# The feed-forward stage of a hybrid decoder step, rebuilt: products in four bank tiles, right operands stored split, and kept sums put back into the banks

## The chip, the cores and the metric

The kernel runs on one core of one Trainium2 chip. The metric is the time of one execution on the device in microseconds (us); lower is better. TensorE is called PE here, its weight loads PEld, VectorE DVE, ScalarE ACT, GpSimd POOL and the sync engine SP, as the profile does.

## The reference, cut to what matters

One layer of a decoder for 512 prompt tokens and 32 sample tokens (544 columns together). The change touches its last block only:

```
hf = rmsnorm(x, norm_ffn_g)
gate, up = split(hf @ w_gate_up, 2)          # 2048 -> 2 x 5632
x = x + (silu(gate) * up) @ w_down           # 5632 -> 2048
```

All is float32. Ahead of it stand the mixers (stick-breaking attention and gated DeltaNet), their output projection and a cross attention; none of that is changed.

## The kernel before, in words

**Products.** The tokens lie as columns: a feature block is a tile of 128 rows by 544 columns, and half of it (272 columns, `HT`) is one half of the tokens. To keep float32 accuracy at the speed of the shorter format `float32r`, each operand is split into two exact parts, `hi` by an ACT copy and `lo` by a DVE subtraction, and a product is three matmuls (hi·hi, hi·lo, lo·hi). On top of that the feed-forward stage uses Winograd's scheme on 2 x 2 blocks: two blocks of weight columns, pairs of feature blocks and the two halves of the tokens give seven products p1 to p7 in place of eight. `wino` (lines 1626 to 1650) runs them: for two pairs at a time it calls `left`, and then issues 7 products x 2 pairs x 3 = 42 matmuls of 128x272. Such a group of 42 is called a step below.

**Left operands.** `left` (lines 1603 to 1623) loads two transfers of 256 KB of weights on SP's queue into a tile `u` (three buffers), makes four sums on POOL (lines 1613 to 1616, 128x256 each), and splits the seven operands in two pieces of 768 and 1024 columns: ACT `wh` (line 1620), DVE `wl` (line 1621). The pieces lie in two pools of two buffers each: the 768 piece holds left operands 0, 1, 2, the 1024 piece 3 to 6. The order of products is p1, p2, p4, p6, p5, p7, p3, which use left operands 1, 2, 0, 4, 3, 5, 6.

**Right operands.** `sums` (lines 1565 to 1576) makes two more tiles from a pair of feature blocks, and `part_of` (lines 1579 to 1592) splits them, so that a pair has seven right operands in seven tiles of 272 KB. `PAIR_TAGS` and `DOWN_PLAN` say in which tiles a pair may lie.

**Banks.** PSUM has eight banks. `wino` takes two tiles of two banks (`mm`: p1, p2 and p6, p5) and three of one bank (`aux`: p4, p7, p3).

**Gate and up.** `ffn` (lines 1682 to 1752) loops over 44 blocks of the hidden features (`j`); each is a `wino` over 8 pairs, so 4 steps. `combine` (lines 1653 to 1680) turns the seven products into gate and up (one ACT copy, seven DVE adds of 128x272 that read a bank), three multiplications on DVE (lines 1712, 1714, 1715) and a Silu on ACT (line 1713) follow. After every second `j` POOL makes the `sums` of the new pair (lines 1572 to 1575), and four transfers on ACT's queue store it, unsplit, in DRAM (`hT`, 7 x 272 columns, lines 1719 and 1721).

**Down.** The 22 pairs of hidden features are taken in chunks of 4, 4, 4, 4 and 6. In a chunk the loop goes over 8 values of `m`, each a `wino` for two blocks of the output: 2 steps, in the last chunk 3. `combine` then adds the chunk's result to two accumulators: one ACT copy, seven DVE adds that read a bank, and two POOL adds of 128x544 (lines 1670 and 1671). `fetch` (lines 1688 to 1699) loads the next chunk's pairs: four transfers on SP's queue (line 1696), seven tiles split by ACT and DVE (lines 1590 and 1591). It is called at m = 4 and m = 10 for one pair each, and at m = 14 for the rest, whose tiles are in use until then. In the last chunk POOL adds the residual x (line 1747), and `store_y` (lines 1767 to 1785) transposes each finished block on PE and stores it.

**Order.** The program is Python that emits instructions; a scheduler orders those of each engine by priority, which is the order of the program unless a block asks for more, and by when their operands and buffers would be free. Each engine then works its list in order: one that waits holds up all behind it.

## Time and profile before

| what | value |
|---|---|
| runs | 3063.03, 3061.66 and 3057.8 us, median 3061.66 us |
| profiled execution | span 3059.9 us, granted PE clock 0.983 |
| feed-forward stage in it | first matmul at 1511.5 us, last one ends at 3048.2 us |
| gate and up | 1511.5 to 2484.3 us: 44 `j`, 176 steps |
| down | 2484.3 to 3048.2 us: 88 steps |
| busy over the span | PE 95%, DVE 70%, POOL 55%, ACT 45% |

A page of the profile shows one execution: busy times by engine, the span in 40 slices, the chain of work that ended last, and the costliest groups of instructions by line. Further views used below cut the span into windows, list who waited for whom, or list the instructions in order of time. Each row names engine, line, operation and tiles; a group ends with its busy time and the mean of one instruction, then with the idle time ahead of it and what ended that.

### The profile page before, as it was taken

How to read it: one execution, taken by the hardware profiler on the slowest of the kernel's cores; microseconds unless marked ns; L12 is line 12 of the kernel's file. 1: busy time of each engine (PE TensorE's matmuls, PEld its weight loads, DVE VectorE, ACT ScalarE, POOL GpSimd, SP SyncE). 2: the span in 40 equal slices, each digit the busy share in tenths (PEclk: the TensorE clock that was granted, in tenths of full speed). 3: DMA queues.
4: the chain of work that ended last, by engine and by line, in shares of the span. 5: the costliest groups of instructions: out<-in, count | busy, mean ns of one | idle time of the engine just before them, and what ended most of it. 6: DMA issues, size and time to landing. Idle time of an engine off the chain costs nothing.

```text
span 3059.9 us, 58347 instructions
## 1 busy us (share of the span) xinstructions
PE 2900.2 (95%) x22118; PEld 2789.1 (91%) x22118; DVE 2134.3 (70%) x3339; ACT 1363.5 (45%) x2600; POOL 1671.8 (55%) x1784
## 2 busy tenths in 40 slices
PE   8999999999999999999799999999999989988898
PEld 7999998889899999999689999999999989988797
DVE  6776775655655655366687777777777888888865
ACT  5544453435645654245543343333333344334333
POOL 3211122312112100032378988898888977999997
PEclk9999999999999999999899999999999999999999
DMA  7323233544535765423434344333434354344343
GB/s 212 95 80 85 75 88 99 144 137 147 173 105 151 227 197 150 127 81 116 161 117 127 118 122 123 121 117 118 125 118 123 116 179 132 110 131 127 119 137 105
DMA packets 619505, 392.67 MB, mean 128 GB/s; under 512 B 36475, under 2 KB 572360, under 8 KB 619224
## 3 DMA queue, kind: packets, MB, share of 16 engines
q1 hardware_dynamic: 596904, 355.95, 39.6%
q10 hardware_dynamic: 22320, 32.99, 3.0%
q8 instruction: 174, 2.85, 0.4%
q14 instruction: 107, 0.88, 0.1%
HBM read 334.17 MB, written 54.68 MB: 127 GB/s over the span
## 4 chain that ended last, share of the span: by engine, by line
POOL 27%; PE 20%; DVE 8%; issue 4%; DMA 4%; ACT 2%; SPq 0%; POOLq 0%; ACTq 0%; DVEq 0%
PE mm L208 7%; POOL u L1615 6%; POOL u L1613 6%; POOL u L1614 5%; PE mm L1647 5%; POOL u L1616 5%; PE aux L1647 4%; DVE wl L1621 3%; DMA u<-in_w_gate_up 2%; DVE pr L1591 2%; PE aux L1342 2%; POOL acc L1670 1%; PE mm L1530 1%; POOL x L1572 1%; PE aux L960 1%
## 5 line engine op out<-in xcount | busy, mean ns | idle before, releaser
L1621 DVE TENSOR_TENSOR wl<-u,wh 128x768 fp32r<-128x768 f32 (+1 forms) x528 | 752.5, 1442 | 315.9 <-ACT wh L1620 213.6
L1647 PE MATMUL mm<-pr,wh 128*128 128x272 f32 x4224 | 830.6, 292 | 41.6 <-DVE acc L1663 25.3
L1620 ACT CAST wh<-u 128x768 fp32r<-128x768 f32 (+1 forms) x528 | 488.8, 943 | 826.5 <-PE aux L1647 295.4
L1647 PEld LDWEIGHTS mm<-pr,wh 128*128 128x128 f32 x4224 | 669.4, 191 | 50.5 <-DVE acc L1663 20.3
L1647 PE MATMUL aux<-pr,wh 128*128 128x272 f32 x3168 | 626.9, 292 | 17.7 <-DVE acc L1669 6.7
L1647 PE MATMUL mm<-pr,wl 128*128 128x272 f32 x2112 | 615.7, 292 | 22.5 <-DVE wl L1621 22.5
L208 PE MATMUL mm<-ah,wh 128*128 128x272 f32 (+1 forms) x2464 | 538.6, 298 | 5.7 <-ACT ah L321 4.6
L1647 PEld LDWEIGHTS aux<-pr,wh 128*128 128x128 f32 x3168 | 506.8, 192 | 21.7 <-DVE acc L1669 8.6
L208 PE MATMUL mm<-al,wh 128*128 128x272 f32 (+1 forms) x2464 | 524.3, 291 | 0.7 <-DVE al L239 0.7
L208 PE MATMUL mm<-ah,wl 128*128 128x272 f32 (+1 forms) x2464 | 515.6, 290 | 0.1
L1647 PE MATMUL aux<-pr,wl 128*128 128x272 f32 x1584 | 460.9, 291 | 2.0 <-DVE wl L1621 2.0
L1647 PEld LDWEIGHTS mm<-pr,wl 128*128 128x128 f32 x2112 | 403.3, 191 | 28.4 <-DVE wl L1621 28.4
L208 PEld LDWEIGHTS mm<-ah,wh 128*128 128x128 f32 (+1 forms) x2464 | 391.9, 189 | 28.8 <-issue 8.5
L197 DVE TENSOR_TENSOR wl<-wr,wh 128x512 fp32r<-128x512 f32 (+1 forms) x366 | 264.0, 725 | 195.9 <-ACT wh L196 186.7
L208 PEld LDWEIGHTS mm<-al,wh 128*128 128x128 f32 (+1 forms) x2464 | 389.6, 188 | 5.4 <-issue 2.0
L208 PEld LDWEIGHTS mm<-ah,wl 128*128 128x128 f32 (+1 forms) x2464 | 386.2, 188 | 2.5 <-DVE wl L197 0.5
L196 ACT CAST wh<-wr 128x512 fp32r<-128x512 f32 (+1 forms) x366 | 224.3, 615 | 336.6 <-PE mm L208 272.6
L1613 POOL TENSOR_TENSOR u<-u 128x256 f32<-128x256 f32 x264 | 277.3, 1050 | 140.8 <-DMA u<-in_w_gate_up 90.2
L1615 POOL TENSOR_TENSOR u<-u 128x256 f32<-128x256 f32 x264 | 323.2, 1224 | 0.0
L1616 POOL TENSOR_TENSOR u<-u 128x256 f32<-128x256 f32 x264 | 308.5, 1169 | 19.1
L1647 PEld LDWEIGHTS aux<-pr,wl 128*128 128x128 f32 x1584 | 303.7, 192 | 2.6 <-DVE wl L1621 2.4
L1614 POOL TENSOR_TENSOR u<-u 128x256 f32<-128x256 f32 x264 | 270.4, 1024 | 0.0
(518 smaller groups left out, 3809.1 us busy)
## 6 DMA issues: line engine op xcount, KB each, us to landing
u<-in_w_gate_up SPq DMA_DIRECT2D x352, 256.0 KB
wr<-in_w_in SPq DMA_DIRECT2D x108, 512.0 KB
u<-in_w_down SPq DMA_DIRECT2D x176, 256.0 KB
v<-hT SPq DMA_DIRECT2D x66, 272.0 KB
page<-in_cache_sb_k SPq DMA_DIRECT2D x128, 128.0 KB
page<-in_cache_sb_v SPq DMA_DIRECT2D x64, 256.0 KB
wr<-in_w_out SPq DMA_DIRECT2D x32, 512.0 KB
hT<-x ACTq DMA_DIRECT2D x44, 272.0 KB
```

What stands on the lines that cost most here:

```text
L196: nc.scalar.copy(hi[:, :m, :n], raw[:, k : k + m, :n])
L197: nc.vector.tensor_sub(lo[:, :m, :n], raw[:, k : k + m, :n], hi[:, :m, :n].bitcast(F32))
L208: c.nc.tensor.matmul(ps[:n, h, :HT], l[:, :n], r[:, h * HT : (h + 1) * HT], start=first and i == 0, stop=last and i == 2,)
L1342: nc.tensor.matmul(ps[:, :256], l, r, start=k == 0 and n == 0, stop=k == 7 and n == 2)
L1591: nc.vector.tensor_sub(lo[:, o : o + n * HT], x[:, : n * HT], hi[:, : n * HT].bitcast(F32))
L1613: nc.gpsimd.tensor_add(s1, a21, a22)
L1614: nc.gpsimd.tensor_sub(s3, a11, a21)
L1615: nc.gpsimd.tensor_sub(s2, s1, a11)
L1616: nc.gpsimd.tensor_sub(s4, a12, s2)
L1620: nc.scalar.copy(hi, u[:, o : o + n])
L1621: nc.vector.tensor_sub(lo, u[:, o : o + n], hi.bitcast(F32))
L1647: nc.tensor.matmul(ps, l[:, cols], r, start=u + i == 0 and j == 0, stop=u + i == n - 1 and j == 2)
```

## The change

1. **Left operands.** Weights and sums get tiles of their own (`raw`, three buffers, and `sum`, two). POOL makes two of the four sums, DVE the other two. The 768 piece is split from `raw` alone.
2. **Banks.** The seven products lie in four tiles that are allocated once: P16 (p1, p6), P7, P45 (p4, p5), P23 (p2, p3). The order of products is p1, p6, p7, p4, p5, p2, p3, so left operands 1, 4, 5, 0, 3, 2, 6. One more bank is left for transposes.
3. **Combination in gate and up.** One ACT copy and five DVE adds (three of 272 columns, two of 544) in place of one and seven.
4. **Right operands of the down projection.** Each pair is split once, before it is stored: ACT makes `hi`, POOL `lo`, and seven transfers of 272 KB on ACT's queue store the tiles. `fetch` is then seven transfers on POOL's queue straight into the operand tiles, and ACT and DVE have no part in it. It asks for the last two pairs of a chunk together.
5. **Accumulation in the down projection.** The seven sums of products of each `m` are kept as they are (`Sums`). After the first chunk ACT puts four of them (P45, P23) back into their banks, and the matmuls add to them; `keep` copies them out again on ACT. P16 and P7 are added on DVE. POOL's two adds by `m` are gone. The combination (`finish`, five DVE adds) runs once, in the last chunk.
6. **Residual.** x is added in the second chunk, with three POOL operations by `m`.

Docstrings and comments, which the change also takes out, are left out here.

```diff
 def left(c, w, k, ca, cb):
-    u = c.wu.tile([P, 8, 2 * P], F32, tag="u", name="u", bufs=3)
+    a, b = (c.wu.tile([P, 4, 2 * P], F32, tag=x, name=x, bufs=n) for x, n in (("raw", 3), ("sum", 2)))
...
-    nc.gpsimd.tensor_add(s1, a21, a22)
-    nc.gpsimd.tensor_sub(s3, a11, a21)
-    nc.gpsimd.tensor_sub(s2, s1, a11)
-    nc.gpsimd.tensor_sub(s4, a12, s2)
+    nc.gpsimd.tensor_sub(b[:, 2], a[:, 0], a[:, 2])
+    nc.gpsimd.tensor_add(b[:, 0], a[:, 0], a[:, 1])
+    nc.vector.tensor_add(b[:, 1], b[:, 2], a[:, 1])
+    nc.vector.tensor_sub(b[:, 3], a[:, 3], b[:, 1])
...
-    todo = ((p1, 1, 0), (p2, 2, 1), (p4, 0, 6), (p6, 4, 4), (p5, 3, 3), (p7, 5, 5), (p3, 6, 2))
+P16, P7, P45, P23 = range(4)
+PRODUCTS = ((P16, 0, 1, 0), (P16, 1, 4, 4), (P7, 0, 5, 5), (P45, 0, 0, 6), (P45, 1, 3, 3), (P23, 0, 2, 1), (P23, 1, 6, 2))
+SEEDED = (P45, P23)
...
+def combine(c, y, z):
+    v = c.nc.vector
+    b, e = c.tt("b"), c.tt("e")
+    s1, u4, u2, u3 = b[:, :HT], b[:, HT:], e[:, :HT], e[:, HT:]
+    c.nc.scalar.copy(s1, c.bank[P16][:, 0])
+    v.tensor_add(u2, s1, c.bank[P16][:, 1])
+    v.tensor_add(u3, u2, c.bank[P7][:, 0])
+    v.tensor_add(u4, u2, c.bank[P45][:, 1])
+    v.tensor_add(halves(z), twice(u3), c.bank[P45])
+    v.tensor_add(halves(y), halves(b), c.bank[P23])
+
+class Sums:
...
+    def seed(self):
+        for p in SEEDED:
+            self.c.nc.scalar.copy(self.c.bank[p], self.parts[p])
+
+    def keep(self, added=False):
+        for p, x in enumerate(self.parts):
+            if added and p not in SEEDED:
+                self.c.nc.vector.tensor_add(x, x, self.c.bank[p])
+            else:
+                self.c.nc.scalar.copy(x, self.c.bank[p])
+
+    def residual(self, y, z):
+        g = self.c.nc.gpsimd
+        g.tensor_add(self.z, self.z, z)
+        g.tensor_add(self.y, self.y, y)
+        g.tensor_sub(self.y[:, HT:], self.y[:, HT:], z[:, HT:])
+
+    def finish(self):
+        v = self.c.nc.vector
+        p1, p6, p7, p5 = self.a[:, :HT], self.a[:, HT:], self.s, self.z[:, HT:]
+        v.tensor_add(p6, p6, p1)
+        v.tensor_add(p7, p7, p6)
+        v.tensor_add(p6, p6, p5)
+        v.tensor_add(halves(self.z), halves(self.z), twice(p7))
+        v.tensor_add(self.y, self.y, self.a)
...
     def fetch(ci, count, got):
-            for i in range(4):
-                n, o = (2, 2 * i - 1) if i else (1, 0)
-                v = c.tk("v") if i % 2 else c.hp.tile([P, T], F32, tag="hv", name="v", bufs=2)
-                nc.sync.dma_start(v[:, : n * HT], src[:, o * HT : (o + n) * HT])
-                part_of(c, v, tags, n, ops)
+            tiles = [operand(c, [tag]) for tag in PAIR_TAGS[DOWN_PLAN[ci][len(got)]]]
+            for i, t in enumerate(tiles):
+                nc.gpsimd.dma_start(t, src[:, i])
...
         if j % 2:
-            dst = hT[j // 2]
-            nc.scalar.dma_start(dst[:, :HT], v[0][:, :HT])
-            for i, x in enumerate((v[1], *sums(c, *v, nc.gpsimd))):
-                nc.scalar.dma_start(dst[:, (2 * i + 1) * HT : (2 * i + 3) * HT], x)
+            tiles = []
+            for i, x in enumerate((*v, *sums(c, *v, nc.gpsimd))):
+                hi, lo, n, _ = part_of(c, x, lambda: c.hp.tile([P, T], F32R, tag="st", name="hs", bufs=4), 2 if i else 1, nc.gpsimd)
+                for t in (hi, lo)[2 - n :]:
+                    nc.scalar.dma_start(hT[j // 2, :, len(tiles)], t[:, :].bitcast(F32))
+                    tiles.append(t)
...
-                if m == KD - 2 and u < 2:
-                    fetch(ci + 1, 1 if len(DOWN_PLAN[ci]) == 4 else 2, nxt)
+                if m == KD - 2 and u == 0:
+                    fetch(ci + 1, 2, nxt)
...
-            p = wino(c, c.w_down, 2 * first[ci], m * P, (m + 1) * P, pairs, step)
             if ci == 0:
-                acc += [c.tt("acc") for _ in range(2)]
+                acc.append(Sums(c, m // 2))
+            else:
+                acc[m // 2].seed()
+            wino(c, c.w_down, 2 * first[ci], m * P, (m + 1) * P, pairs, step, 0, SEEDED if ci else ())
+            acc[m // 2].keep(ci > 0)
+            if ci == 1:
+                x = [c.cst.tile([P, T], F32, tag="rstd", name="xl", bufs=2) for _ in range(2)]
+                for i in range(2):
+                    nc.sync.dma_start(x[i], c.xT[m + i])
+                acc[m // 2].residual(*x)
             if last:
-                x = c.wu.tile([P, 2, T], F32, tag="u", name="xl", bufs=3)
-                nc.sync.dma_start(x, c.xT[m : m + 2].rearrange("k p t -> p k t"))
-                for i in range(2):
-                    nc.gpsimd.tensor_add(acc[m + i], acc[m + i], x[:, i])
-            combine(c, p, *acc[m : m + 2], None if ci == 0 else nc.vector if last and m == KD - 2 else nc.gpsimd)
-            if last:
-                done = [(m + i, acc[m + i]) for i in range(2)]
+                acc[m // 2].finish()
+                done = [(m, acc[m // 2].y), (m + 1, acc[m // 2].z)]
...
+    banks = ctx.enter_context(tc.tile_pool(name="banks", bufs=1, space=PSUM))
+    c.bank = [banks.tile([P, n, 512], F32, name=f"bank{i}")[:, :, :HT] for i, n in enumerate((2, 1, 2, 2))]
+    c.aux = lambda: banks.tile([P, 512], F32, tag="aux", name="aux", bufs=1)
     ffn(c, pairs, st, r1)
```

More of the change, by code (lines that the diff above doesn't have):

```diff
@@ L1646, in wino @@
                 for j, (l, r) in enumerate(((wh, bh), (wh, bl), (wl, bh))):
-                    nc.tensor.matmul(ps, l[:, cols], r, start=u + i == 0 and j == 0, stop=u + i == n - 1 and j == 2)
+                    nc.tensor.matmul(
+                        c.bank[p][:, o], l[:, cols], r,
+                        start=u + i == 0 and j == 0 and p not in seeded, stop=u + i == n - 1 and j == 2,
+                        skip_group_check=p in seeded,
+                    )
         if step:
             step(u // 2)
-    return p1, p2, p3, p4, p5, p6, p7
```

97 lines of the change are left out of this document (38 added, 59 removed).

## The prediction, made blind

> **What bounds the kernel now.** I read the page first, then windows along the stages, then who waited for whom, then the groups by shape. A step is 42 matmuls, a `j` of gate and up 4 steps, an `m` of the down projection 2 (3 in the last chunk).
>
> ```profile
> PE 2900.2 (95%) x22118; PEld 2789.1 (91%) x22118; DVE 2134.3 (70%) x3339; ACT 1363.5 (45%) x2600; POOL 1671.8 (55%) x1784
> POOL 27%; PE 20%; DVE 8%; issue 4%; DMA 4%; ACT 2%; SPq 0%; POOLq 0%; ACTq 0%; DVEq 0%
> ```
>
> PE is busiest over the span, yet the chain that ended last runs through POOL more than through PE. The windows say where (PE, PEld, DVE, ACT, POOL busy; then granted clock, DMA share, GB/s):
>
> ```profile
> 1511.50:1596.80 85.30, 72.23 (x513) 69.70 (x514) 72.56 (x91) 45.75 (x70) 61.93 (x58) 0.92 0.41 127
> 1596.80:2484.30 887.50, 870.91 (x6890) 864.29 (x6889) 685.82 (x744) 342.92 (x418) 792.84 (x736) 1.00 0.40 122
> 1877.30:1899.30 22.00, 21.25 (x170) 21.00 (x169) 16.33 (x19) 8.19 (x10) 18.28 (x19) 1.00 0.43 133
> 1899.30:1920.40 21.10, 21.10 (x170) 21.10 (x169) 16.81 (x19) 8.40 (x10) 20.79 (x19) 1.00 0.37 109
> 2484.30:2582.30 98.00, 88.00 (x675) 86.27 (x674) 84.53 (x113) 45.87 (x65) 77.46 (x72) 0.97 0.50 150
> 2582.30:2677.10 94.80, 88.85 (x674) 87.66 (x673) 80.48 (x101) 39.68 (x55) 85.11 (x73) 0.96 0.42 123
> 2633.60:2644.10 10.50, 10.50 (x86) 10.50 (x85) 8.79 (x13) 4.16 (x5) 10.42 (x9) 1.00 0.37 108
> 2677.10:2785.10 108.00, 90.96 (x675) 88.86 (x673) 94.86 (x111) 42.37 (x60) 105.38 (x85) 0.93 0.43 126
> 2785.10:2887.60 102.50, 89.65 (x672) 87.69 (x672) 88.36 (x106) 40.23 (x57) 99.26 (x82) 0.95 0.42 125
> 2887.60:3048.20 160.60, 146.21 (x1074) 140.96 (x1075) 102.76 (x117) 60.47 (x111) 142.28 (x119) 0.94 0.43 126
> 3048.20:3059.90 11.70, 3.04 (x16) 2.20 (x14) 4.48 (x10) 3.58 (x13) 0.00 (x0) 0.67 0.25 74
> ```
>
> Row 7 is one undisturbed `m`: two steps in 10.50 us, 5.25 a step, the pace of PE's matmuls. At that pace the first three `j` would take 63 us (row 1: 85.3), the other 41 would take 861 (row 2: 887.5, 21.65 each; an even `j` 22.0 and an odd one 21.1, rows 3 and 4), and the 88 steps of the down projection 462 (rows 5, 6 and 8 to 10: 563.9). So the matmuls are at their pace in gate and up, and the excess of 102 us lies in the down projection, at a clock of 0.93 to 0.97 with POOL almost without a pause (99.26 of 102.5). After the last matmul 11.7 us are left.
>
> **POOL's relief.** Its groups from 2582.3 to 2887.6 us, chunks 1 to 3:
>
> ```profile
> L1613 POOL TENSOR_TENSOR u<-u 128x256 f32<-128x256 f32 x48 | 47.6, 991 | 8.7 <-DMA u<-in_w_down 7.5 <-DVE acc L1669 1.2
> L1614 POOL TENSOR_TENSOR u<-u 128x256 f32<-128x256 f32 x48 | 57.8, 1204 | 0.0
> L1615 POOL TENSOR_TENSOR u<-u 128x256 f32<-128x256 f32 x48 | 55.8, 1163 | 0.0
> L1616 POOL TENSOR_TENSOR u<-u 128x256 f32<-128x256 f32 x48 | 51.6, 1076 | 3.8
> L1670 POOL TENSOR_TENSOR acc<-acc,a 128x544 f32<-128x544 f32 x23 | 49.0, 2130 | 0.0
> L1671 POOL TENSOR_TENSOR acc<-acc,b 128x544 f32<-128x544 f32 x23 | 35.4, 1540 | 3.0 <-DVE b L1668 3.0
> ```
>
> Four adds twice and the two accumulations make 2 x 4.43 + 3.67 = 12.5 us for an `m` that PE does in 10.5: POOL can't make up for any delay. After the change two adds a step are left, 4.9 us at the dearest mean, in the second chunk three operations more (about 2 x 2.1 + 1.2). POOL stops being the bound there.
>
> **DVE's load in gate and up** is the price. What a moved add costs is bounded by the same add of 272 columns on both engines, and by a DVE group that always met POOL and one that never did:
>
> ```profile
> L1613 POOL TENSOR_TENSOR u<-u x264: 716/742/1866, 1489.6 to 3031.1; 128x256 f32<-128x256 f32 x132
> L1572 DVE TENSOR_TENSOR x<-v x8: 430/435/1024, 1481.6 to 1541.7; 128x272 f32<-128x272 f32 x8
> L1675 DVE TENSOR_TENSOR g<-b,mm x44: 419/430/432, 1550.7 to 2492.5; 128x272 f32<-128x272 f32 x44
> L1714 DVE TENSOR_TENSOR u<-u,rstd x44: 1247/1258/1270, 1553.3 to 2495.0; 128x544 f32<-128x544 f32 x44
> L1670 DVE TENSOR_TENSOR acc<-acc,a x1: 721/721/721, 3051.9 to 3051.9; 128x544 f32<-128x544 f32 x1
> L1621 DVE TENSOR_TENSOR wl<-u,wh 128x1024 fp32r<-128x1024 f32 x264 | 415.0, 1572 | 254.2 <-ACT wh L1620 152.4 <-POOL u L1614 96.4 <-PE aux L1647 4.2
> L1621 DVE TENSOR_TENSOR wl<-u,wh 128x768 fp32r<-128x768 f32 x264 | 346.5, 1312 | 61.7 <-ACT wh L1620 61.2
> ```
>
> With a bank as one input the duration never varies (419 to 432 ns); with two tiles of SBUF it lies between 430 and 1024, and 544 columns take 721 ns at the end, where POOL has no work, against 1258 beside it. So the two engines hold each other up. From 430 and 721 a column costs 1.07 ns, so 768 and 1024 columns undisturbed about 0.96 and 1.24 us (estimates); the means hold 0.35 and 0.33 us of waiting. That is 2.7 us a `j`, with the multiplications about 4.
>
> A `j` gains eight DVE adds: 3.4 us at 0.43, 8.2 at 1.02. POOL's own work at its cheapest falls from 16 x 0.73 + 1.5 (a pair's sums, as two such adds) = 13.2 us to 8 x 0.73 + 1.5 + 2.7 (the new `lo` parts, 952 columns a `j` at 0.73 for 256) = 10.0, so I let DVE's waits shrink by a quarter, 1.0 us, and take 0.6 for an add, near its undisturbed row: 4.8. The new combination takes 3 x 0.43 + 2 x 0.72 against 7 x 0.43, 0.3 less. From 16.8 (row 4): 16.8 + 4.8 - 1.0 - 0.3 = 20.3 of 21.0. DVE is then nearly full, and it works in order:
>
> ```profile
> ACT wh L1620 <- POOL x L1575: 134.1, 18, 7.7
> DVE wl L1621 <- ACT wh L1620: 108.6, 132, 2.6
> ```
>
> (waits in row 2's window.) The first is the even `j`: the store of the sums sits in ACT's queue waiting for POOL, with the next weights' casts behind it, up to 7.7 us. Seven stores that wait for POOL's `lo` parts replace four; POOL is freer. I let half of the 1 us go. The new order of products also frees the 768 piece after 36 of 42 matmuls in place of 18, so a late split has 6.0 us before PE needs it where it had 8.3, and the 1024 piece 6.0 for 7.5. For that and the fuller DVE I add 0.25 us: 21.5 a `j`, 881.5 for 41. Bounds: 21.0, and 16.8 + 8.2 - 0.3 = 24.7. The first three `j` stay at 85.3: the same splits of the tokens fill them.
>
> Two-tile DVE operations and POOL exclude each other in the Trainium skill too, for the whole of an instruction (SBUF — State Buffer, section "Who interferes with whom"). By that rule with undisturbed durations an odd `j` would have needed 13.2 + 8.8 + 2.2 = 24.2 us; the trace has 21.1, so only part of each instruction excludes the other. Taken as it stands it gives 24 after the change as well (10.0 + 8.8 + 2.2 + 3.4), so 21.65 would stay and the sum would be 6 us higher.
>
> **The put-back sums.** ACT's copies:
>
> ```profile
> L1661 ACT COPY g<-mm x44: 377/386/388, 1545.4 to 2487.0; 128x272 f32<-128x272 f32 x44
> L1713 ACT ACTIVATE g<-g x44: 647/652/660, 1554.6 to 2496.7; 128x544 f32<-128x544 f32 x44
> PE mm L1647 <- DVE acc L1663: 25.3, 12, 7.4
> ```
>
> No row writes a bank from ACT; I take 0.65 us for 544 columns in either direction, as the second row, which is nearest; 0.39 for half of them bounds it below, the last rival but one above. P45 ends 12 matmuls (1.5 us) before the `m` does and is wanted 18 (2.25) into the next: 3.75 us for 1.3 us of copies. P23 has 30 matmuls, 3.75 us too. One pair of casts ahead of them (8.40 us a `j`, so 2.1 a step at most) still fits: 3.4. They are hidden; if not, each of 32 `m` waits. In exchange PE's waits for the accumulation (third row, down projection) go: P16 is complete 30 matmuls before the end.
>
> **The fetch at a chunk's start.** Two pairs, 14 tiles of 272 KB, 3.9 MB, must come between the end of the last `m`'s first step and the second step of the next chunk: 10.5 us.
>
> ```profile
> q1 hardware_dynamic: 596904, 355.95, 39.6%
> q10 hardware_dynamic: 22320, 32.99, 3.0%
> ACT pr L1590 <- DMA v<-hT: 36.7, 20, 6.2
> 2677.10:2699.40 22.30, 13.94 (x87) 13.21 (x85) 21.93 (x25) 9.00 (x14) 22.06 (x17) 0.77 0.56 163
> ```
>
> q10 carried these long rows: 32.99 MB in 3.0% of the span, 359 GB/s when working; q1 mostly weights, 294. So 10.9 us, 3.6 for two steps of weights, 1.8 for the landing (third row, mean): 16.3, 5.8 late, and 2 us for the slow clock after a pause (fourth row: 0.77): 8 a chunk. Chunk 0 needs four pairs and waits 10. The last needs four as well, 10, and in seven of its `m` the transposes stay:
>
> ```profile
> 3008.42 0.63 PE L960 MATMUL aux<-ident,acc 128*128 128x128 f32 x4
> 3009.03 0.40 PE L1781 MATMUL aux<-ident,acc 128*32 128x128 f32 x2
> 3010.44 0.52 PE L1647 MATMUL aux<-pr,wh 128*128 128x272 f32 x2 [1.01 <-DVE acc L1669]
> ```
>
> From 3008.35 to 3010.44 no product runs, with four more transposes 2.4 us, of which 1.0 is a wait that I keep, since one bank is left for them. Of the 14 issues for the two early pairs of a chunk (m = 4 and 10) nothing shows: POOL has 5 us free in each `m`. The stores grow from 0.95 to 1.9 MB for two `j`, 23 GB/s at a DMA share of 0.40; hidden. Down: 94 + 3 x 92 + (126 + 10 + 16) = 522, against 563.9.
>
> **End and sum.** Behind the last matmul seven adds of 0.43 and two of 0.72 become one copy and one add: 11.7 - 3.0 = 8.7. 1511.5 + 85.3 + 881.5 + 522 + 8.7 = 3009.0, 50.9 under the span of 3059.9. The runs' median, 3061.66, less that is 3010.8.
>
> **Rivals.** DVE becomes the bound of gate and up: an add at 0.73, the middle of its bounds, no relief in the old waits, and half of the 2.6 us a `j` that it waits for ACT stay: 16.8 + 5.8 - 0.3 + 1.3 = 23.6, so 3097; it ends slower than before from 22.75 a `j` on, 3142 at 24.7. For it speaks 20.3 of 21.0, against it POOL's lighter load.
>
> The fetch through POOL's queue is no faster than the old path: each issue holds POOL and the adds behind it, waits for a tile to come free included. SP's issue takes about 0.34 us; at 1.2 us 14 take 17, and each start costs about 9 more: 3056. In the Trainium skill a transfer from this queue takes 2.0 us and its bytes at 436 GB/s (DMA: Bandwidth & Descriptors, "Anatomy of one DMA — SWDGE (gpsimd) path"), 2.6 us for a tile; 14 without overlap would be 37 us. No run here shows one.
>
> The put-back holds PE: a copy behind casts that themselves wait for PE, 1.9 us for 32 `m`: 3072.
>
> Everything hides: 21.1 a `j`, 4 us a start, the first `j` 10 us shorter: 2965.
>
> **Numbers.** Forecast 0.44, all hidden 0.18, DVE 0.20, POOL's queue 0.12, put-back 0.06. A measurement of this kernel can tell about 0.2%, 6 us. Faster: 0.44 + 0.18 + most of POOL's queue, 0.70; same 0.07; slower 0.23. The range reaches from all hidden, 2960, into the DVE case, 3090; alone the forecast has 2985 to 3040.
>
> **What would show it.** Down windows near 92 us with POOL well under 90% busy and a clock near 1; no wait of PE on an accumulation. Gate and up: DVE above 90%, a `j` near 21.5. Wrong, if a `j` takes over 22.5 with PE waiting for `wl`, if PE waits for the fetched tiles over 10 us a chunk, or if it waits for ACT's copies at each `m`.

## The result and the profile after

After takes 3131.11 us (median of 4 runs, 3128.71 to 3132.79), before in the same series 3062.35 (4 runs): a ratio of 1.0231, 95% interval 1.0216 to 1.0246. That is slower by 2.3%, outside the forecast's range and on its other side. The profiled execution of after has a span of 3131.0 us, 71.1 more than before's.

The page of after, busy times and the chain that ended last:

```profile
PE 2925.2 (93%) x22118; PEld 2814.3 (90%) x22118; DVE 2168.3 (69%) x3513; ACT 1441.3 (46%) x2720; POOL 1042.2 (33%) x1444
PE 36%; DVE 12%; POOL 7%; issue 4%; DMA 4%; ACT 2%; ACTq 0%; SPq 0%; POOLq 0%; DVEq 0%
```

POOL lost 630 us of work and its share of the chain fell from 27% to 7%, as meant. Still the kernel is slower, so shares over the span can't tell why. The windows by stage can (PE, PEld, DVE, ACT, POOL busy; granted clock, DMA share, GB/s): first three `j`; `j` 3 to 42; one even `j`; one odd `j`; the last `j`; chunks 0 to 4; what follows the last matmul.

```profile
1514.40:1602.20 87.80, 74.19 (x513) 71.80 (x514) 72.16 (x106) 43.64 (x67) 42.48 (x41) 0.91 0.34 107
1602.20:2567.20 965.00, 888.88 (x6723) 878.34 (x6722) 773.11 (x963) 377.38 (x481) 441.81 (x480) 0.96 0.41 129
2009.00:2036.00 27.00, 23.06 (x170) 22.62 (x169) 20.69 (x25) 10.09 (x14) 14.82 (x15) 0.94 0.45 142
2036.00:2057.10 21.10, 21.10 (x171) 21.10 (x169) 18.11 (x25) 8.76 (x12) 7.50 (x10) 1.00 0.38 112
2567.20:2602.20 35.00, 23.51 (x170) 23.21 (x169) 18.51 (x22) 8.83 (x12) 23.07 (x40) 0.80 1.07 309
2602.20:2696.30 94.10, 87.81 (x675) 87.14 (x674) 62.26 (x70) 48.42 (x68) 44.06 (x63) 0.95 0.57 166
2696.30:2789.70 93.40, 87.47 (x675) 84.90 (x674) 79.72 (x78) 46.58 (x65) 65.40 (x76) 1.00 0.69 202
2789.70:2882.70 93.00, 86.78 (x675) 86.40 (x674) 63.51 (x80) 46.57 (x65) 43.11 (x66) 0.96 0.67 192
2882.70:2970.40 87.70, 85.57 (x674) 84.36 (x674) 63.73 (x80) 46.69 (x65) 39.63 (x62) 1.00 0.64 185
2970.40:3118.80 148.40, 137.57 (x1076) 135.69 (x1075) 108.51 (x153) 72.97 (x129) 41.64 (x61) 0.95 0.47 137
3118.80:3131.00 12.20, 3.21 (x16) 1.57 (x14) 2.06 (x4) 3.94 (x13) 0.00 (x0) 0.71 0.24 71
```

The balance against before, in us: start of gate and up +2.9, first three `j` +2.5, `j` 3 to 42 +99 (965.0 against 865.8), the last `j` +13.3 (35.0 against 21.7), down projection -47.3 (516.6 against 563.9), end +0.5: together 71. The odd `j` is undisturbed (21.1, clock 1.00). The loss is in the even `j`, right after a pair is complete: 27.0 us against 22.0, twenty times. It lies in the third of the four steps, 11.3 us in place of 6.3 (means of the twenty).

Who waited for whom in `j` 3 to 42 (engine and line, releaser, us in total, times, longest), of PE, ACT and POOL:

```profile
PE bank L1654 <- ACT wh L1624: 55.9, 20, 3.2
ACT hs L1594 <- POOL hs L1595: 114.7, 40, 4.9
POOL sum L1617 <- DVE wl L1625: 498.3, 160, 5.6
```

Twenty waits of PE for ACT's cast of the weights (and 22, 20.0 us in all, for VectorE's split of them), forty of ACT for a low part that POOL makes. The timeline of `j` 20 shows how the two hang together (start, us, engine, line, operation; in brackets the idle time before it). POOL, then ACT, then PE:

```profile
2014.84 1.16 POOL L1617 TENSOR_TENSOR sum<-raw 128x256 f32<-128x256 f32 x1 [5.37 <-DVE wl L1625]
2015.95 0.74 POOL L1618 TENSOR_TENSOR sum<-raw 128x256 f32<-128x256 f32 x1
2016.65 0.95 POOL L1573 TENSOR_TENSOR x<-u 128x272 f32<-128x272 f32 x1
2017.57 0.95 POOL L1574 TENSOR_TENSOR x<-u,x 128x272 f32<-128x272 f32 x1
2018.60 1.37 POOL L1575 TENSOR_TENSOR x<-u,x 128x272 f32<-128x272 f32 x1
2019.93 1.33 POOL L1595 TENSOR_TENSOR hs<-u,hs 128x544 fp32r<-128x544 f32 x1
...
2016.11 5.51 ACTq L1760 DMA_DIRECT2D hT<-hs  x2
2021.66 0.64 ACT L1594 CAST hs<-x 128x544 fp32r<-128x544 f32 x1 [4.85 <-POOL hs L1595]
2022.21 1.04 ACT L1624 CAST wh<-sum 128x1024 fp32r<-128x1024 f32 x1
...
2023.30 0.52 PE L1654 MATMUL bank<-pr,wh 128*128 128x272 f32 x2 [2.91 <-ACT wh L1624]
```

Read it backwards. PE waits at 2023.30 for the cast at 2022.21. The sums were ready (VectorE's last add of them ended at 2017.89), but the cast stands in ACT's queue behind two stores, and the second store waits 5.5 us for a low part that POOL finishes at 2021.26. POOL had been idle for 5.37 us before 2014.84; then sums of weights, three of the pair's sums and the low part came all at once. The load of no engine shows this: POOL is busy 14.82 of 27.00 us.

Before has the same wait in ACT's queue, and a longer one. A row of its timeline, from `j` 22:

```profile
2018.18 3.47 ACT L1620 CAST wh<-u 128x1024 fp32r<-128x1024 f32 x4 [7.44 <-POOL x L1575]
```

What differs is when it ends. From the first matmul of an even `j` to the weights' cast behind the long store it is 11.1 us in before and 13.4 in after (means of the twenty), while the third step begins at 10.5 in both. PE idles 0.8 us in an even `j` of before and 3.8 in one of after. The other 2.0 of the 5 us are in the matmuls themselves: behind the pause they ran at a lower granted clock, 0.77 in the row below and 1.00 in the odd `j`, and PE is busy 23.06 us in this `j` against 21.10 in the next.

```profile
2023.30:2030.75 7.45, 6.42 (x37) 6.20 (x37) 5.97 (x5) 3.11 (x4) 3.45 (x5) 0.77 0.45 161
```

The last `j` is another matter, also on POOL: it issues transfers of the fetch, many of which wait for their tile, and the next weights' sums stand behind them (the first and the last row of those that hold the 28 issues, the sum behind them, and PE's wait in that `j`):

```profile
2568.01 1.30 POOL L1735 DMA_DIRECT2D pr<-hT  x2 [1.76 <-PE bank L1654]
...
2590.96 0.53 POOL L1735 DMA_DIRECT2D pr<-hT  x1 [0.24 <-DMA pr<-hT]
2591.50 0.73 POOL L1617 TENSOR_TENSOR sum<-raw 128x256 f32<-128x256 f32 x1
...
PE bank L1654 <- ACT wh L1624: 11.5, 1, 11.5
```

### The profile page after: what moved, and what is told of

Read it like the earlier page. It is cut to its first block, busy times and chain, and to the rows that moved or that the text cites. A ratio compares the mean times of both kernels' runs of the same rounds, so it can differ in the third digit from the quotient of the medians.

```text
span 3131.0 us, 58882 instructions
## 1 busy us (share of the span) xinstructions
PE 2925.2 (93%) x22118; PEld 2814.3 (90%) x22118; DVE 2168.3 (69%) x3513; ACT 1441.3 (46%) x2720; POOL 1042.2 (33%) x1444
## 3 DMA queue, kind: packets, MB, share of 16 engines
q1 hardware_dynamic: 584360, 334.50, 36.8%
## 4 chain that ended last, share of the span: by engine, by line
PE 36%; DVE 12%; POOL 7%; issue 4%; DMA 4%; ACT 2%; ACTq 0%; SPq 0%; POOLq 0%; DVEq 0%
PE bank L1654 24%; PE mm L208 7%; DVE wl L1625 6%; POOL sum L1617 2%; PE aux L1342 1%; DVE sum L1619 1%; DMA raw<-in_w_gate_up 1%; DMA raw<-in_w_down 1%; POOL hs L1595 1%; PE mm L1530 1%; ACT wh L1624 1%; POOL x L1575 1%; PE aux L960 1%; DMA pr<-hT 1%; POOL x L1573 1%
## 5 line engine op out<-in xcount | busy, mean ns | idle before, releaser
L1654 PE MATMUL bank<-pr,wh 128*128 128x272 f32 x7392 | 1444.0, 295 | 105.3 <-ACT wh L1624 88.4
L1654 PEld LDWEIGHTS bank<-pr,wh 128*128 128x128 f32 x7392 | 1196.8, 194 | 115.5 <-ACT wh L1624 96.5
L1654 PE MATMUL bank<-pr,wl 128*128 128x272 f32 x3696 | 1089.4, 295 | 30.3 <-DVE wl L1625 30.1
L1654 PEld LDWEIGHTS bank<-pr,wl 128*128 128x128 f32 x3696 | 717.7, 194 | 38.8 <-DVE wl L1625 38.0
L1617 POOL TENSOR_TENSOR sum<-raw 128x256 f32<-128x256 f32 x264 | 221.4, 839 | 786.4 <-DVE wl L1625 748.3
L1625 DVE TENSOR_TENSOR wl<-sum,wh 128x1024 fp32r<-128x1024 f32 x264 | 334.3, 1267 | 105.6 <-ACT wh L1624 103.6
L1624 ACT CAST wh<-raw 128x768 fp32r<-128x768 f32 x264 | 220.0, 833 | 366.2 <-PE bank L1654 328.1
L1619 DVE TENSOR_TENSOR sum<-sum,raw 128x256 f32<-128x256 f32 x264 | 233.8, 886 | 164.3 <-POOL sum L1617 164.1
L1625 DVE TENSOR_TENSOR wl<-raw,wh 128x768 fp32r<-128x768 f32 x264 | 280.0, 1061 | 73.2 <-ACT wh L1624 46.7
L1624 ACT CAST wh<-sum 128x1024 fp32r<-128x1024 f32 x264 | 277.2, 1051 | 104.6 <-DVE sum L1620 95.0
L1618 POOL TENSOR_TENSOR sum<-raw 128x256 f32<-128x256 f32 x264 | 209.4, 793 | 0.0
L1735 POOL DMA_DIRECT2D pr<-hT x154 | 83.0, 551 | 33.1 <-PE bank L1654 16.6
```

The source lines that it names most:

```text
L1617: nc.gpsimd.tensor_sub(b[:, 2], a[:, 0], a[:, 2])
L1618: nc.gpsimd.tensor_add(b[:, 0], a[:, 0], a[:, 1])
L1619: nc.vector.tensor_add(b[:, 1], b[:, 2], a[:, 1])
L1624: nc.scalar.copy(hi, x)
L1625: nc.vector.tensor_sub(lo, x, hi[:, :, :].bitcast(F32))
L1654: nc.tensor.matmul(c.bank[p][:, o], l[:, cols], r, start=u + i == 0 and j == 0 and p not in seeded, stop=u + i == n - 1 and j == 2, skip_g ...
```

## The experiments

Durations are taken from each run's profiled execution: a `j` from its first matmul to the next one's (mean of the twenty even ones from 4 to 42, of the twenty odd ones from 3 to 41), the down projection as a whole. Ratios are to before, measured beside each run. In the diffs `...` marks what is left out, and comments are added here.

| run | us | ratio, 95% interval | even `j` | odd `j` | last `j` | down |
|---|---|---|---|---|---|---|
| before (profiled) | 3062.35 | 1 | 22.2 | 21.1 | 21.7 | 563.9 |
| after | 3131.11 | 1.0231 (1.0216-1.0246) | 27.2 | 21.1 | 35.1 | 516.6 |
| x1_stores_pool | 3137.16 | 1.0270 (1.0253-1.0287) | 27.0 | 21.9 | 36.3 | 513.8 |
| x2_stores_sp | 3119.99 | 1.0207 (1.0190-1.0224) | 26.0 | 22.1 | 36.3 | 514.2 |
| x3_order | 3207.74 | 1.0497 (1.0479-1.0514) | 26.4 | 24.7 | 36.8 | 535.3 |
| x4_lo_dve | 3064.46 | 1.0020 (1.0009-1.0031) | 24.0 | 21.3 | 37.6 | 515.4 |
| y1_lo_dve_st_sp | 3080.64 | 1.0074 (1.0054-1.0094) | 24.2 | 21.9 | 35.9 | 514.4 |
| y7_spread | 3143.14 | 1.0275 (1.0253-1.0297) | 27.2 | 21.8 | 35.4 | 517.3 |
| y5_left_dve_at_fetch | 3054.54 | 0.9991 (0.9981-1.0002) | 24.0 | 21.3 | 24.6 | 516.8 |
| y4_fetch_sp | 3054.85 | 0.9995 (0.9986-1.0004) | 24.0 | 21.3 | 33.8 | 508.4 |
| y6_no_putback | 3137.23 | 1.0257 (1.0236-1.0278) | 27.2 | 21.1 | 34.7 | 526.4 |
| z1_sum3 | 3341.86 | 1.0935 (1.0918-1.0952) | 29.4 | 24.3 | 21.2 | 625.5 |
| x6_left_pool | 3197.35 | 1.0461 (1.0446-1.0477) | 29.3 | 21.1 | 38.1 | 536.9 |
| z3_mix | 3043.36 | 0.9960 (0.9947-0.9973) | 23.6 | 21.1 | 24.4 | 516.7 |
| w1_no_lo | 3080.18 | 1.0082 (1.0066-1.0097) | 24.2 | 22.2 | 36.4 | 507.8 |
| z4_lo_in_place | 3114.71 | 1.0192 (1.0178-1.0206) | 26.6 | 21.4 | 28.4 | 515.3 |
| z6_fetch_sp | 3049.34 | 0.9965 (0.9953-0.9977) | 23.5 | 21.1 | 21.1 | 522.3 |
| v1_whole | 3034.17 | 0.9923 (0.9910-0.9936) | 23.8 | 21.1 | 25.0 | 501.5 |
| v2_whole_pool | 3036.01 | 0.9922 (0.9909-0.9935) | 23.9 | 21.1 | 24.4 | 503.3 |

**First theories: a queue, the buffers, or VectorE.** The stores moved to SyncE's queue:

```diff
-                    nc.scalar.dma_start(hT[j // 2, :, len(tiles)], t[:, :].bitcast(F32))
+                    nc.sync.dma_start(hT[j // 2, :, len(tiles)], t[:, :].bitcast(F32))
```

> The same stores issued from SP's queue, where the loads of the weights stand. Queue theory: ACT is free as in the kernel with the stores on POOL's queue, but now the weights' loads wait behind stores that wait for POOL's lo parts; three raw buffers cover about two steps (10.5 us), so between 3030 us (covered) and 3090 (half of the stall moves to the loads). DVE theory and buffer theory: about 3131.

The even `j` kept 26.0 us, and the odd one rose by 1.0. PE's long wait for ACT's cast is gone, and its third step falls from 11.3 us to 8.5. But the weights' cast still stands behind ACT's cast of the pair, which waits for POOL's sums, and VectorE's split behind it takes 2.17 us beside POOL's low parts (1.22 where POOL is idle). PE waits for that split, 1.69 us in each of the twenty. In `j` 10 of this run:

```profile
1773.12 0.65 ACT L1594 CAST hs<-x 128x544 fp32r<-128x544 f32 x1 [1.73 <-POOL x L1574]
1773.67 1.04 ACT L1624 CAST wh<-sum 128x1024 fp32r<-128x1024 f32 x1
1774.75 2.17 DVE L1625 TENSOR_TENSOR wl<-sum,wh 128x1024 fp32r<-128x1024 f32 x1 [0.85 <-ACT wh L1624]
1775.80 3.62 POOL L1595 TENSOR_TENSOR hs<-x,hs 128x544 fp32r<-128x544 f32 x2
1776.98 0.59 PE L1654 MATMUL bank<-pr,wl 128*128 128x272 f32 x1 [1.69 <-DVE wl L1625]
```

On SyncE's queue the stores hold raw weights besides: POOL waited for these 20 times, 69.6 us in all, and the fourth step and the next odd `j` got longer.

The stores on POOL's own queue (x1_stores_pool, the same line with `nc.gpsimd`) were to bring 100 us if ACT's queue was the cause. The even `j` kept 27.0 us; PE's waits are for VectorE's splits here too, among them 1.69 us at the same place in all twenty. That the store's wait in ACT's queue is the whole cause fell with these two runs. What they leave is that the weights' casts and splits stand behind work of the pair that waits for POOL; neither run takes all of that away.

An order of the products like that of before, in which the 768 piece is used up earlier:

```diff
-PRODUCTS = ((P16, 0, 1, 0), (P16, 1, 4, 4), (P7, 0, 5, 5), (P45, 0, 0, 6), (P45, 1, 3, 3), (P23, 0, 2, 1), (P23, 1, 6, 2))
+PRODUCTS = ((P16, 0, 1, 0), (P45, 0, 0, 6), (P23, 0, 2, 1), (P16, 1, 4, 4), (P7, 0, 5, 5), (P45, 1, 3, 3), (P23, 1, 6, 2))
```

> The changed kernel with the products in another order (p1, p4, p2, then p6, p7, p5, p3), so that the 768 piece is free after 18 of 42 matmuls again, as before the change, and a late split has 8.3 and 7.5 us in place of 6.0. Buffer theory: the even j comes back to about 22 us, 3030. Queue theory: the stall of 6 us shrinks by the 1.5 to 2.3 us of slack, 20 x 2 = 40 us less, 3090. DVE theory: 3131. In the down projection the banks have less time between their last and their next matmul, which may cost some us there.

The even `j` gained 0.8 us, every odd one lost 3.6. In this run PE waits for no cast and no split of the weights in gate and up, although these come as late as in after (13.8 us from the start of an even `j`). Its waits are for banks:

```profile
PE bank L1654 <- DVE e L1673: 110.1, 38, 5.0
```

So going back to an earlier order doesn't bring the 5 us back, since the lateness reaches PE by VectorE's combination instead. But the time that an order leaves until PE wants a late piece does decide whether it waits for it; the buffer theory is not refuted as a part of the cause.

The low parts of the stored pairs on VectorE:

```diff
-... "st", name="hs", bufs=4), 2 if i else 1, nc.gpsimd)
+... "st", name="hs", bufs=4), 2 if i else 1, nc.vector)
```

> The changed kernel with the lo parts of the stored pairs made by DVE in place of POOL (1904 columns for two j, about 2.7 to 4.5 us). Queue theory: the first three stores of a pair no longer wait for POOL, the last four still wait for POOL's sums: an even j falls by about half of the stall, 24 us, so about 3070. DVE theory: DVE gets fuller and the even j longer, 3150 or more.

67 us come back by giving the engine said to be nearly full more work: the whole loss against before but 0.2%. So VectorE was not the bound, and the engine that makes the low parts decides most of it. The mechanism stays, but shorter: in `j` 20 of this run ACT's first two stores wait 3.35 us in place of 5.51, and the weights' casts go on after 11.6 us in place of 13.4. The third step still takes 7.0 to 9.2 us.

With the low parts on VectorE and the stores on SyncE's queue as well (y1_lo_dve_st_sp) the even `j` is no better, 24.2, and the time 3080.64 us: POOL now waits for raw weights, 20 times, 72.2 us in all.

**The order of the same work.** The pair's sums, parts and stores handed out in four pieces, one behind each of the next four steps:

```diff
-            for i, x in enumerate((*v, *sums(c, *v, nc.gpsimd))):
...
+            later = pair_out(c, hT, j // 2, v)     # a generator of four pieces
...
+        def step(u):
+            next(later, None)
```

> After with the same instructions on the same engines and queues; only their order is changed: the stored pair's second half (sums, casts, low parts, stores) is not issued in one piece behind the pair, but in four pieces, one behind each of the next j's four weight steps. Burst theory (eight instructions in one piece stand in POOL's and ScalarE's in-order queues ahead of the next steps' weight sums and weight casts): an even j falls from 27.1 us to 21.3 to 22.3, about twenty of them, 3131 - 20 x 5.3 = 3020 to 3035; j 43 and the chunk starts stay. Capacity theory (POOL, at 14.8 us busy of an even j's 27, or VectorE has no room wherever the work stands): nothing moves, 3125 to 3135, or the loss goes over to the other three steps. Theory of the buffers (four st buffers for seven stored tiles, each waiting for a landed store): spreading gives the stores time, so it would also fall, but to 23 to 24: 3060 to 3075.

Nothing was gained. POOL's low parts now lie apart, with weight sums between them, yet the first store still waits 5.51 us and the cast behind it is as late (`j` 22 of this run, ACT):

```profile
2067.02 5.51 ACTq L1731 DMA_DIRECT2D hT<-hs  x2
2072.58 1.04 ACT L1624 CAST wh<-sum 128x1024 fp32r<-128x1024 f32 x1 [4.85 <-POOL hs L1595]
```

The first three sums and the first low part still came in one piece, so the theory was half tested: what it says of the later pieces is refuted, what it says of the first is not touched.

**More buffers for the weight sums**, three in place of two:

```diff
-    a, b = (... for x, n in (("raw", 3), ("sum", 2)))
+    a, b = (... for x, n in (("raw", 3), ("sum", 3)))
```

> After with three buffers in place of two for the weight sums; the room comes from letting three operand tiles of one gate/up pair share one tile, so that part of the operands (and so of the result) is overwritten; the number of instructions and matmuls is that of after. Before had three buffers for raw blocks and sums together, after has three for the raw blocks but two for the sums, and POOL waits 5.4 us per j for a sum buffer just ahead of the burst. Lookahead theory (the third step's sums could have been made in that wait, and then the burst would hit nothing): even j falls from 27.1 to 22 to 23.5, 3131 - 20 x 4 = 3040 to 3060. Queue theory (ScalarE's casts stand behind stores that wait for POOL's low parts, whatever is ready ahead): an even j falls by 2 us at most, 3085 to 3131.

Both theories missed: 3341.86 us, every stage but the last `j` slower. The down projection says nothing on buffers here: the three operand tiles that share one are also tiles that a fetch fills, so its transfers can have to wait for one another. `j` 3 to 42 have no such transfers, and took 1073.6 us in place of 965.0. POOL and VectorE waited there:

```profile
POOL sum L1621 <- DMA raw<-in_w_gate_up: 496.3, 90, 8.2
DVE sum L1623 <- POOL sum L1621: 286.3, 140, 4.6
```

With room for a further sum, VectorE's queue holds the sum of a later step ahead of the low part of the current one, and so waits for weights that are still loading, while their buffer waits for VectorE. The waits are shown; that this order is their cause is read from one stretch of the timeline, and was not tested by itself.

**The split of the weight sums.** All four on POOL again, nothing else changed:

```diff
-    nc.vector.tensor_add(b[:, 1], b[:, 2], a[:, 1])
-    nc.vector.tensor_sub(b[:, 3], a[:, 3], b[:, 1])
+    nc.gpsimd.tensor_add(b[:, 1], b[:, 2], a[:, 1])
+    nc.gpsimd.tensor_sub(b[:, 3], a[:, 3], b[:, 1])
```

> After with the first part undone alone: all four weight sums on POOL, everywhere, as in the kernel before; the low parts of the stored pairs stay on POOL. If POOL's work in an even j is the cause (14.8 us busy there, and 8 x 0.8 more make 21.2 of 21.1): even j 28 to 30, and the down projection loses part of its 47 us, since POOL then carries four sums a step: 3170 to 3230. If the cause is that the sums now pass from POOL to VectorE, which adds a wait of POOL and one of VectorE to every step, and not the low parts: even j back to 22 to 24, 3050 to 3090.

Slower by another 66 us: 2.1 in each even `j`, 20 in the down projection. With the low parts on POOL, the split of the sums is needed.

**The put-back**, taken out: VectorE adds all kept sums.

```diff
-SEEDED = (P45, P23)
+SEEDED = ()
```

> After without the put-back: all kept sums are added to their banks' products by VectorE, none is put back by ScalarE. It prices the part that the change is named for. If the put-back only moves work that is hidden either way (VectorE is busy 63.7 of a chunk's 87.7 us, and 2 x 0.71 us an output pair more make it 75): 3125 to 3137. If the bank's release behind four adds in a row is late for the next output pair's matmuls: 0.6 to 1 us for each of 32 output pairs, 3150 to 3163. If the put-back itself costs: down to 3110.

The ratio's interval overlaps after's; the profile has 9.8 us more in the down projection (526.4), 5.4 of them in chunk 3. The part that gave the change its name is worth about 10 us at most, and costs nothing.

**The last `j` and the chunk starts.** On top of x4_lo_dve, VectorE makes POOL's two sums in the last `j` and in the first and last `m` of each chunk:

```diff
+    eng = eng or nc.gpsimd          # nc.vector if j == NH - 1, or m in (0, KD - 2)
-    nc.gpsimd.tensor_sub(b[:, 2], a[:, 0], a[:, 2])
-    nc.gpsimd.tensor_add(b[:, 0], a[:, 0], a[:, 1])
+    eng.tensor_sub(b[:, 2], a[:, 0], a[:, 2])
+    eng.tensor_add(b[:, 0], a[:, 0], a[:, 1])
```

> The kernel with the low parts on VectorE (3064), and also, in the three kinds of blocks around a fetch of stored pairs (the last j, and the first and last output pair of each chunk), the two weight sums that POOL makes are made by VectorE, so that no weight sum stands behind POOL's transfer issues. Theory that POOL's in-order queue makes the loss there (j 43 37.6 us in place of 21.1, the second step of chunk 2's and chunk 4's first output pair 8 and 13 us too long): j 43 falls to 22 to 26, the chunk starts to within 3 us, together 20 to 30 us: 3035 to 3045. Theory that the raw weights land late beside the fetch's transfers: j 43 stays over 32, and under 8 us come back: 3056 to 3064. VectorE being overrun instead (2 x 0.8 us more in each of those steps) would show as steps of 5.5 to 6 us in all of those blocks: 3060 to 3075.

The last `j` falls from 37.6 to 24.6: POOL's queue was most of the cause there. The down projection doesn't fall (516.8 against 515.4), so there the theory failed: PE's waits for ACT's casts shrink from 15.6 us to 2.1, but it now waits longer for VectorE's additions to the kept sums (7.3 us, 3.7 in x4_lo_dve) and for the fetched tiles themselves (3.4 there, here):

```profile
PE bank L1655 <- DMA pr<-hT: 8.4, 6, 4.9
```

On top of x4_lo_dve again, with the sums left on POOL and the fetches on SyncE's queue:

```diff
-                nc.gpsimd.dma_start(t, src[:, i])
+                nc.sync.dma_start(t[:, :].bitcast(F32), src[:, i])
```

> After with the low parts on VectorE (alone 3064) and the fetches of stored pairs on SyncE's queue in place of POOL's, so that no weight sum on POOL stands behind a fetch. If POOL's queue makes the loss at the last j (37.6 us against 21.3) and at the chunk starts: j 43 under 26, chunk 2 and 4 each 5 us shorter, 3035 to 3050. If the raw weight loads, now behind fetches that wait for their tiles in SyncE's queue, are late instead: j 43 30 or more and chunks of 95 to 100, 3065 to 3090.

The down projection gains 7 us, the last `j` only 3.8, because raw weights now stand behind the fetches: SyncE issues 26 of them from 2504.58 to 2524.28, and the next raw block at 2524.66, for which POOL waits until 2531.49.

**Mixing engines.** Low parts on VectorE, all four weight sums of gate and up on POOL, and y5's sums around the fetches:

```diff
+        wino(..., eng=(nc.vector,) if j == NH - 1 else (nc.gpsimd, nc.gpsimd))   # engines of the first and last two sums
```

> Low parts of the stored pairs on VectorE; in gate/up all four weight sums on POOL (as in the kernel before), which gives VectorE 1.3 to 1.7 us of every step back; around the fetches the POOL sums on VectorE as in the run that gave 3054.5; the rest of the down projection as in after. If what is left of an even j's loss there (23 to 25 us against 21.1) is VectorE, full in the third step: even j 21.5 to 22.5, 3005 to 3025. If POOL's four weight sums with the pair's four sums make a new burst: even j 23 to 25 again or more, 3050 to 3075. The last j and the chunk starts stay at the values of the 3054.5 run (24.6 us; 8 us each, PE waiting for fetched tiles).

Faster than before by 0.4%, but the even `j` stayed at 23.6: VectorE's load was not what was left. In the profile its low part of the pair waits for ACT's cast, 2.07 us at 1985.62, with the weights' low part behind it. z6_fetch_sp puts the fetches of chunks 1 to 4 on SyncE's queue, and POOL's two sums of the down projection back on POOL:

> The kernel that gave 3043 with the fetches for chunks 1 to 4 from SyncE's queue and POOL's two weight sums back on POOL in the down projection. If POOL's queue made part of the chunk starts' loss: the down projection 505 to 510 in place of 516.7, 3030 to 3038. If the fetched data are late whoever asks for them: 3040 to 3047. If raw weights now wait behind fetches: 3050 or more.

No gain (0.9965 against 0.9960): chunks 2 and 3 fell by 7 and 3 us, but the first step of chunk 0 took 26.7 us in place of 6.9, more than the last `j` gained (21.1 in place of 24.4). That wait only moved.

**The low parts left out** (high parts stored twice in their place, so that the down projection lacks the low ones; stores and buffers stay, and ACT makes one more copy of 272 columns for each pair):

```diff
-                hi, lo, n, _ = part_of(...)
-                for t in (hi, lo)[2 - n :]:
...
+                nc.scalar.copy(hi[:, : T if i else HT], x[:, : T if i else HT])
...
+                for t in (hi, hi)[: 2 if i else 1]:
```

> After without the low parts of the stored pairs: the subtraction is left out and the high part is stored twice, so that the seven stores, their queue and their four buffers stay and the operands of the down projection are wrong. If the low parts on POOL are the cause (they hold ScalarE's stores and casts, and POOL's next weight sums): even j 21.1 to 22.5, 3131 - 20 x 5 = 3020 to 3045 (the last j and the chunk starts keep their loss). If the stores or their buffers are the cause: even j 25 to 27, 3100 to 3131.

51 us come back, less than by moving the low parts to VectorE. Between the cases: the low parts on POOL are most of it, as far as this run separates them, but the casts and stores in ACT's queue still wait for POOL's sums and for landed stores, with the weights' casts behind them (`j` 3 to 42):

```profile
ACT hs L1759 <- POOL x L1574: 34.8, 20, 1.7
ACT wh L1624 <- DMA hT<-hs: 12.3, 5, 2.9
```

**The low part written over its own input** (z3_mix with fewer buffers needed):

```diff
...
+                    nc.scalar.copy(hi, x)
+                    nc.vector.tensor_sub(x, x, hi[:, :].bitcast(F32))
...
```

> The kernel that gave 3043 (low parts on VectorE, the four weight sums of gate/up on POOL), with the low part written over the value that it is taken from and stored from there, so that a pair takes four of the four stored buffers in place of seven, and no cast on ScalarE waits for a store to land. Theory that the rest of an even j's loss (23.5 to 25.0 against 21.06) is the casts' wait for a buffer (in that run VectorE waits 2.07 us for the cast hs, with the weights' low parts behind it): even j 21.1 to 22.5, 3000 to 3025. If it is POOL's burst of weight sums and the pair's sums: unchanged, 3038 to 3050.

Slower by 71 us than z3_mix. To overwrite `u`, VectorE must first wait for all of POOL's sums that read it, with the weights' low parts behind:

```profile
DVE u L1762 <- POOL x L1575: 98.1, 20, 4.9
```

**The one part undone.** Everything of after is kept, except that a pair is stored whole, and split when it is fetched:

```diff
+                nc.scalar.dma_start(hT[j // 2, :, max(0, 2 * i - 1) * HT : (2 * i + 1) * HT], x[:, : (2 if i else 1) * HT])
...
+                nc.sync.dma_start(lo.bitcast(F32), src[:, max(0, 2 * i - 1) * HT :][:, : n * HT])
+                nc.scalar.copy(hi, lo.bitcast(F32))
+                nc.vector.tensor_sub(lo, lo.bitcast(F32), hi.bitcast(F32))
```

> After with one part undone: an even j's pair is stored whole (four stores from ScalarE's queue, as in the kernel before), and split into high and low parts when the down projection fetches it (four loads on SyncE's queue, four casts on ScalarE, four subtractions on VectorE, in place). Weight sums, banks, put-back stay as in after. If storing parts is the cause: even j 21.1 to 22.5 as before (22.1), the last j under 26, the down projection 516 to 535 because of the splits, 3131 - 100 - 10 + 0 to 20 = 3015 to 3045. If the split of the weight sums between POOL and VectorE is what stalls the even j: even j 24 or more, 3060 to 3110.

3034.17 us: 97 faster than after, and 0.8% faster than before. Its even `j`, its odd `j` and its down projection:

```profile
1972.40:1996.20 23.80, 21.89 (x171) 21.23 (x170) 18.02 (x24) 8.26 (x11) 9.24 (x12) 1.00 0.39 124
1996.20:2017.30 21.10, 21.10 (x170) 21.10 (x170) 18.12 (x26) 8.51 (x11) 6.57 (x10) 1.00 0.40 117
2516.30:3017.80 501.50, 483.48 (x3762) 475.67 (x3763) 417.56 (x538) 297.47 (x459) 178.24 (x202) 0.99 0.47 143
```

VectorE's work in the even `j` is near that of the odd one, and the clock is 1.00. The down projection, which now does the splits that after had moved out of it, is 15 us shorter than after's. With all four weight sums of gate and up on POOL as well:

> The same as v1_whole with all four weight sums of gate/up on POOL, which is the gate/up of the kernel before but for the banks. If the split of the sums is worth nothing in gate/up, where nothing but the pair's sums shares POOL: equal to v1_whole within 6 us. If VectorE was the tighter engine: 10 to 25 us faster than v1_whole. If POOL's sums in a row (3.2 us a step) are late: even j 23 or more, 10 to 30 us slower than v1_whole.

The same time within 2 us: once pairs are stored whole, the split of the weight sums matters nothing in gate and up.

## Why the prediction was wrong

**The step that failed** is in VectorE's paragraph: "Seven stores that wait for POOL's `lo` parts replace four; POOL is freer. I let half of the 1 us go." It gave every even `j` 0.5 us back; the change took 5.0 from it, twenty times. The step saw the wait (134.1 us, 18 times, in before) and the queue behind it, and then judged by POOL's load. The wait is a latency: POOL can't go on with the pair before the second `u` is there, and then a store needs three sums and a low part in a row, 2016.65 to 2021.26, 4.6 us, where in before it needed the sums alone. So the weights' casts behind it come 2.3 us later. No rival had this either: VectorE's case would have ended slower, but by another cause. v1_whole, with that part undone and the rest kept, shows it for the part as a whole (97 us, the last `j` and the fetch among them).

**The slack** is the term beside it: "For that and the fuller DVE I add 0.25 us." In v1_whole the casts come after 10.7 us, no later than in before, and PE still idles 1.6 us in an even `j` where it idled 0.8; with the slower matmuls behind it that is the 1.6 us by which its even `j` exceeds before's. v2_whole_pool has the four sums on POOL, as before has, and the same even `j`, so these 1.6 us belong to the order of products, the banks and their tiles; no run separates those. By these readings the 5.0 us are some 2.3 for the later cast, 0.7 for the smaller slack and 2.0 for the matmuls behind the pause. That split is an estimate from the means of before, after and v1_whole; no run takes the three apart.

**The last `j`** was not priced at all: the forecast let chunk 0 wait 10 us, but the four pairs' 28 issues fall into the last `j`, ahead of weight sums. 13.3 us, most of it by POOL's queue (y5). The second rival had named the mechanism, "each issue holds POOL and the adds behind it", but priced it at the chunk starts alone.

**VectorE's load**: 20.3 us a `j` forecast, 19.3 on average (773.11 over 40; 18.1 in an odd `j`, 20.7 in an even one), so it was not nearly full. The adds took more than assumed, the old waits shrank far more (adds; splits of 1024 and of 768 columns; a multiplication, in `j` 3 to 42):

```profile
L1619 DVE TENSOR_TENSOR sum<-sum,raw 128x256 f32<-128x256 f32 x161 | 141.5, 879 | 88.4 <-POOL sum L1617 88.4
L1620 DVE TENSOR_TENSOR sum<-raw,sum 128x256 f32<-128x256 f32 x160 | 120.2, 752 | 3.4
L1625 DVE TENSOR_TENSOR wl<-sum,wh 128x1024 fp32r<-128x1024 f32 x160 | 200.8, 1255 | 86.8 <-ACT wh L1624 86.8
L1625 DVE TENSOR_TENSOR wl<-raw,wh 128x768 fp32r<-128x768 f32 x160 | 168.5, 1053 | 12.5 <-PE bank L1654 10.9 <-ACT wh L1624 1.5
L1752 DVE TENSOR_TENSOR u<-u,rstd 128x544 f32<-128x544 f32 x40 | 28.8, 719 | 0.7
```

0.82 for an add in place of 0.6, but 1.26 and 1.05 for the splits (1.57 and 1.31 before) and 0.72 for each of the three multiplications (0.92 for one and 1.26 for two before): 2.3 + 1.3 = 3.6 us of the 4 went, not 1.0.

**Down projection**: 522 forecast, 516.6 measured, and term by term 94.1, 93.4, 93.0, 87.7, 148.4 against 94, 92, 92, 92, 152. POOL's relief was right: it is busy 39.63 of chunk 3's 87.70 us. That the price of the chunk starts came out is luck. The forecast blamed late data, and PE waited for fetched tiles 1.3 us in all; it waited 16.6 us for ACT's casts, at the starts of chunks 2 and 4, where the weights' sums stood behind POOL's issues, and 6.3 us for ACT's copies in chunk 0. In chunk 1 it isn't the start that is long, but the second step of every `m`, 5.9 to 7.3 us beside the residual's operations on POOL. When POOL's queue was cleared (y5), the down projection took as long, with longer waits for tiles and for VectorE.

**Put-back**: hidden, as forecast. ACT's copies took 0.62 and 0.61 us for 544 columns, 0.65 assumed, and an undisturbed `m` has 10.5 us:

```profile
L1694 ACT COPY bank<-a 128x544 f32<-128x544 f32 x48 | 29.6, 616 | 0.8
L1702 ACT COPY a<-bank 128x544 f32<-128x544 f32 x48 | 29.2, 609 | 72.2 <-PE bank L1654 72.2
```

**The end**: 8.7 forecast, 12.2 measured. The adds did shrink (VectorE 4.48 to 2.06 us), but the last stores run one behind the other: transposes, ACT, a landed store of 2.29 us on the chain, transposes again. That the single bank left for transposes makes them do so was not tested.

**Slips that change nothing**: four adds at 1.204 us are 4.8, not 4.9; everything hiding comes to about 2960, as the range has it, not 2965; and the 1.2 us for an issue from POOL stood in no row (0.55 was measured).

## What to carry to other kernels

Work taken off a full engine has to be put into queues, and there its latency counts, not its load: ask for each instruction that waits for another engine what stands behind it on its own, and how soon PE needs that. Parts that nobody needs for hundreds of microseconds should not be finished in the loop that feeds PE, if finishing them takes a chain over three engines; stored whole and split when fetched, the same work was free here. And when a change has several parts, one run that undoes each is worth more than an argument over the sum: here the sum of the other parts (v1_whole, 0.8% faster) was hidden under one bad one. And a wait that grows is judged by when it ends: before had a longer one in the same queue, which ended 2.3 us earlier against PE's need.

## What the runs showed of the hardware

- A transfer issued from POOL took 0.55 us of POOL for each 272 KB tile (mean of 154); its median time to landing beside other traffic was 5.8 us. By the Trainium skill (DMA: Bandwidth & Descriptors, "Anatomy of one DMA — SWDGE (gpsimd) path"), cited in the prediction, a tile alone would take 2.6 us, an estimate from the page's figures; no run has one alone. The 28 tiles of the last `j` took 23.5 us of issues with their waits, and 309 GB/s moved in that `j` with the weights beside them.
- ACT wrote 544 columns into a pair of banks in 0.62 us, and matmuls went on adding to what it had put there.
- Leaving instructions out (w1_no_lo, 3080) was slower than giving them to the fuller engine (x4_lo_dve, 3064), and a third buffer was slower than two (z1_sum3: 1073.6 us for `j` 3 to 42, 965.0 in after): the place of waiting instructions in the queues outweighed both work and room.
